# Adaptive max pooling: a full load of 64 KB rows comes first, the short load of 8 KB rows second

## The chip, the cores and the metric

The kernel runs on one core of a Trainium2 chip. The metric is the device time in microseconds (us) of one execution; the median of three runs is 335.33 us. All data is float32. Of the core's engines only VectorE (DVE in the profile) computes; SyncE (SP) and ScalarE (ACT) issue transfers, which 16 DMA engines carry out.

## The reference

```python
batch, channels, length = 32, 256, 4096
output_size = 256

def reference(x, output_size):
    result = np.zeros((batch, channels, output_size), dtype=np.float32)
    for i in range(output_size):
        start = int(i * length / output_size)
        end = int((i + 1) * length / output_size)
        result[:, :, i] = np.max(x[:, :, start:end], axis=-1)
    return result
```

The length is a multiple of the output size, so every output is the maximum of a window of 16 consecutive numbers. 134.2 MB are read and 8.4 MB written, each once.

## The kernel before

The input is seen as 2,097,152 windows of 16 floats (64 bytes each), and the 128 partitions share them: 16,384 windows a partition. They form two groups. In group A each partition owns 15,436 consecutive windows, in group B 948 (`last`).

Group A is loaded in pieces, and the list `group_a` (line 42) gives their sizes in windows a partition: 972, then fourteen of 1024 (`CHUNK`), then 128 (`FIRST`). The loop of line 79 takes the list backwards, and the position `a` goes down with it: so the first transfer is the short load, 128 partitions with rows of 128 x 64 = 8,192 bytes each, from the end of each partition's stretch. Fourteen full loads with rows of 65,536 bytes follow, then the one of 972 windows, then group B's 948. This text counts the loads of line 95 as load 0, load 1 and so on; the short load of line 86 is not among them. All are issued by SyncE, in the order of the program, into one queue.

The tile `ring` has two halves of 1176 windows (`CHUNK + GAP`), and the loads of line 95 take them in turn. Inside its half a load lies at the bottom (windows 0 to 1023) or 152 windows higher (windows 152 to 1175, `moved`): loads 0 and 1 at the bottom, loads 2 and 3 higher, loads 4 and 5 at the bottom again. The short load goes to windows 1024 to 1151 of the first half, above load 0.

VectorE reduces what has landed, in the order of the program: each load of 1024 windows in two instructions of line 55, one of 872 windows and one of 152. The first covers the windows that the load after next will overwrite, so the load after next waits for it and not for the second. Load 2, which lies over windows 152 to 1175 of the first half, also overwrites the place of the short load, so it waits for the short load's reduction too. Each load is waited for by its own semaphore.

The maxima of group A go to the tile `kept`. When all of it is there, SyncE issues one large store of it (line 115). The last load's 948 maxima overwrite the end of its own place in `ring`, and ScalarE issues their small store (line 112).

Of the kernel before, what the change touches and what calls it, by code (L numbers as in the profile page):

```python
# [1 line left out]

# [4 lines left out]


@with_exitstack
def kernel(  # L10
    ctx: ExitStack,
    tc: tile.TileContext,
    x: bass.AP,
    output_size: bass.AP,
    out: bass.AP,
):

    nc = tc.nc
    P = nc.NUM_PARTITIONS
    fp32 = mybir.dt.float32

    B, C, L = x.shape
    O = int(output_size)  # L30
    assert L % O == 0, (L, O)
    W = L // O
    total = B * C * O // P
    assert B * C * O % P == 0

    CHUNK = 1024
    GAP = 152
    FIRST = 128
    LOADS = 14

    last = 948
    group_a = [total - last - LOADS * CHUNK - FIRST] + [CHUNK] * LOADS + [FIRST]
    group_b = [last]
    assert FIRST < group_a[0] <= CHUNK and last * (W + 1) <= CHUNK * W

    pool = ctx.enter_context(tc.tile_pool(name="pool", bufs=1))
    ring = pool.tile([P, 2 * (CHUNK + GAP) * W], fp32, tag="ring", name="ring")
    kept = pool.tile([P, total - last], fp32, tag="kept", name="kept")

    xw = x.flatten_outer_dims().rearrange("r (o w) -> (r o) w", w=W)  # L50
    ow = out.flatten_outer_dims().rearrange("r o -> (r o)")

    def pooled(dst, at, n):

        nc.vector.reduce_max(  # L55
            out=dst,
            in_=ring[:, at * W : (at + n) * W].rearrange("p (n w) -> p n w", w=W),
            axis=mybir.AxisListType.X,
        )

    taken = 0

    def group(n):

        nonlocal taken
        span = slice(taken * P, (taken + n) * P)
        taken += n
        return (
            xw[span].rearrange("(p n) w -> p (n w)", p=P),
            ow[span].rearrange("(p n) -> p n", p=P),  # L70
        )

    stores = []
    n_loads = 0
    base = 0
    for g, loads in enumerate((group_a, group_b)):
        xg, og = group(sum(loads))
        a = sum(loads) if g == 0 else 0
        for n in loads[::-1]:
            if g == 0:  # L80
                a -= n
            xn = xg[:, a * W : (a + n) * W]
            dst = kept[:, base + a : base + a + n] if n != last else None
            if n == FIRST:

                nc.sync.dma_start(  # L86
                    out=ring[:, CHUNK * W : (CHUNK + n) * W], in_=xn
                )
                pooled(dst, CHUNK, n)
            else:  # L90

                low = n_loads % 2 * (CHUNK + GAP)
                moved = n_loads // 2 % 2
                at = low + moved * GAP
                nc.sync.dma_start(out=ring[:, at * W : (at + n) * W], in_=xn)  # L95
                if n != last:
                    cut = CHUNK - GAP if moved else GAP
                    parts = [(0, cut), (cut, n)]
                    for u, v in parts if moved else parts[::-1]:
                        pooled(dst[:, u:v], at + u, v - u)  # L100
                else:
                    end = (at + CHUNK) * W
                    last_kept = ring[:, end - n : end]
                    pooled(last_kept, at, n)
                n_loads += 1
            if g:
                a += n
        if g == 0:
            stores.append((og, kept[:, :]))
    assert taken == total  # L110

    nc.scalar.dma_start(out=og, in_=last_kept)
    tc.no_sync_barrier()
    for dst, src in stores:
        nc.sync.dma_start(out=dst, in_=src)


# [1 line left out]
_INS = ['x', 'output_size']  # L119
_OUTS = [((32, 256, 256), 'float32')]  # L120

_NUMBERS = {'output_size': 256}


# [26 lines left out]
```

## Time and profile before

| what | value |
|---|---|
| median of 3 runs | 335.33 us (335.17 to 335.75) |
| the profiled execution | 335.17 us, of which the span from first to last instruction is 333.4 us |
| VectorE: one full load in two instructions | 17.28 us |
| short load, from issue to landing | 4.7 us |
| full load, from issue to landing (median of 14) | 24.0 us |
| mean rate over the span | 428 GB/s |
| VectorE idle before reductions, waiting for loads | 52.2 us in 17 waits |

The profile shows one execution, with times in microseconds from the start of the span. Its page gives the busy time of each engine, then the span in 40 equal slices in which each digit is the busy share in tenths; then the DMA queues with packets, megabytes and the time of their packets as a share of the time of 16 engines. `L55` is line 55 of the kernel. `SPq` and `ACTq` stand for the instructions with which SyncE and ScalarE issue transfers. `kept<-ring 128x872 f32<-128x13952 f32` is an instruction that writes 872 numbers on each of 128 partitions from 13,952. The chain is the work that ended last, followed back from the last instruction, at each step to what released it.

### The profile page before, as it was taken

To read this page: it belongs to the slowest core of one execution; us is meant where nothing else is said; L and a number is where in the kernel's file an instruction comes from. 1 tells how busy PE (TensorE), PEld (TensorE's weight loads), DVE (VectorE), ACT (ScalarE), POOL (GpSimd) and SP (SyncE) were. 2 spreads that over 40 slices of the span, in tenths; PEclk is the share of its full clock that TensorE was granted. 3 is DMA by queue.
4 is the path that set the end of the run, shared out by engine and by line. 5 is a ranking of instruction groups with operands and counts; after the bars stand their busy time and mean duration, and the time that the engine had idled before them with its cause. 6 is when DMAs were issued, how large, how long until landed. Compare 5 with 4: busy or idle time off the path is not lost.

```text
span 333.4 us, 112 instructions
## 1 busy us (share of the span) xinstructions
DVE 276.6 (83%) x32; POOL 0.2 (0%) x4
## 2 busy tenths in 40 slices
DVE  2009979797997979799797979989797998989894
POOL 0000000000000000000000000000000000000000
DMA  9898989899898989899898989899998989999987
GB/s 377 377 503 377 503 377 503 377 425 456 377 503 377 503 377 503 377 456 425 377 503 377 503 377 503 377 488 393 393 488 377 503 377 478 411 417 466 450 378 295
DMA packets 2736, 142.61 MB, mean 428 GB/s; under 512 B 304, under 2 KB 304, under 8 KB 432
## 3 DMA queue, kind: packets, MB, share of 16 engines
q1 hardware_dynamic: 2592, 142.12, 98.7%
q10 hardware_dynamic: 144, 0.49, 0.5%
HBM read 134.22 MB, written 8.39 MB: 428 GB/s over the span
## 4 chain that ended last, share of the span: by engine, by line
DMA 62%; DVE 36%; SPq 0%; issue 0%; DVEq 0%
DMA ring<-in_x_dram 62%; DVE kept L55 31%; DVE ring L55 5%; SPq L95 0%; SPq L86 0%; DVEq L55 0%
## 5 line engine op out<-in xcount | busy, mean ns | idle before, releaser
L55 DVE TENSOR_REDUCE kept<-ring 128x872 f32<-128x13952 f32 (+3 forms) x31 | 260.6, 8447 | 50.5 <-DMA ring<-in_x_dram 50.5
L55 DVE TENSOR_REDUCE ring<-ring 128x948 f32<-128x15168 f32 x1 | 16.0, 15953 | 1.6 <-DMA ring<-in_x_dram 1.6
L132 POOL MEMSET const-bfloat16-1.0<- 128x1 bf16 x1 | 0.1, 101 | 0.0
L132 POOL MEMSET const-uint8-127<- 128x1 uint8 x1 | 0.1, 101 | 0.0
L132 POOL MEMSET const-float32-0.0<- 128x1 f32 x1 | 0.1, 98 | 0.2 <-issue 0.2
L132 POOL MEMSET const-float32-1.0<- 128x1 f32 x1 | 0.1, 98 | 0.0
## 6 DMA issues: line engine op xcount, KB each, us to landing
ring<-in_x_dram SPq DMA_DIRECT2D x1, 7776.0 KB, 23.0
out_dram<-kept SPq DMA_DIRECT2D x1, 7718.0 KB, 19.8
ring<-in_x_dram SPq DMA_DIRECT2D x1, 7584.0 KB, 21.6
ring<-in_x_dram SPq DMA_DIRECT2D x1, 1024.0 KB, 4.7
out_dram<-ring ACTq DMA_DIRECT2D x1, 474.0 KB, 3.8
ring<-in_x_dram SPq DMA_DIRECT2D x14, 24.0
```

Of the source, the lines that this page charges most:

```text
L55: nc.vector.reduce_max(out=dst, in_=ring[:, at * W : (at + n) * W].rearrange("p (n w) -> p n w", w=W), axis=mybir.AxisListType.X,)
L132: nc = _bacc.Bacc("TRN2", target_bir_lowering=False, num_devices=1)
```

## The change

The list of sizes is built without the short load at its end, and the short load is put in ahead of the list's last element:

```diff
-    group_a = [total - last - LOADS * CHUNK - FIRST] + [CHUNK] * LOADS + [FIRST]
+    group_a = [total - last - LOADS * CHUNK - FIRST] + [CHUNK] * LOADS
+    group_a.insert(-1, FIRST)
```

Read backwards, as the loop does, the list now gives 1024, 128, then thirteen times 1024, 972. Load 0 is issued first and takes the last 1024 windows of each partition's stretch; the short load comes second and takes the 128 windows below them; load 1 and all later loads take the windows that they took before. The places in `ring` stay as they were: load 0 at windows 0 to 1023 of the first half, the short load at 1024 to 1151, load 1 at the bottom of the second half. On VectorE the order is now: load 0's two reductions, the short load's, load 1's two, and on as before. Load 2 waits, as before, for the first part of load 0's reduction and for the short load's reduction, of which the latter now comes last. The lines behind line 42 move down by one.

## The prediction

> **What bounds the kernel now.** I read the page first: the busy shares, the row of slices and the queues.
>
> ```profile
> span 333.4 us, 112 instructions
> DVE 276.6 (83%) x32; POOL 0.2 (0%) x4
> DMA  9898989899898989899898989899998989999987
> q1 hardware_dynamic: 2592, 142.12, 98.7%
> ```
>
> VectorE (DVE) works 276.6 of 333.4 us. The transfers of SyncE's queue (q1: all loads and the large store) fill 98.7% of the time of the 16 DMA engines, and no slice falls under 7 tenths. So transfers bound the kernel, and an edit costs only what makes the engines idle or slow. Next, the instructions in order of time and the chain that ended last:
>
> ```profile
> 0.73 0.36 SPq L86 DMA_DIRECT2D ring<-in_x_dram  x1
> 5.44 2.29 DVE L55 TENSOR_REDUCE kept<-ring 128x128 f32<-128x2048 f32 x1 [5.44 <-DMA ring<-in_x_dram]
> 24.79 17.28 DVE L55 TENSOR_REDUCE kept<-ring 128x872 f32<-128x13952 f32 x2 [17.06 <-DMA ring<-in_x_dram]
> 44.14 17.28 DVE L55 TENSOR_REDUCE kept<-ring 128x872 f32<-128x13952 f32 x2 [2.07 <-DMA ring<-in_x_dram]
> ...
> 311.17 0.35 SPq L115 DMA_DIRECT2D out_dram<-kept  x1
> ```
>
> ```profile
> 1.62 42.50 DMA ring<-in_x_dram
> 44.12 0.02 issue
> 44.14 14.70 DVE kept L55
> 58.84 0.02 issue
> 58.85 23.98 DMA ring<-in_x_dram
> ...
> 291.07 21.61 DMA ring<-in_x_dram
> ```
>
> In each row of the first fence the first number is the start, the second the time. Full loads land 19.35 us apart (24.79 to 44.14): 8,388,608 bytes at 433.5 GB/s. VectorE needs 17.28 us for each and waits some 2.07 us for the next. The chain names VectorE for 14.70 us of each second load because the load after next may not be issued before the first part of a reduction has freed its half of the ring; that step has cover, as the next view shows.
>
> ```profile
> 39.50 0.33 SPq L95 DMA_DIRECT2D ring<-in_x_dram  x1
> ```
>
> This is SyncE's own list around 39.5 us: the third full load (I count full loads 0, 1, 2) is issued 0.02 us after the reduction from 24.79 ends (24.79 + 14.69 = 39.48), and load 1 lands only at 44.12. So load 2 stands in the queue with a lead of 44.12 - 39.50 = 4.62 us, and the engines pass from load 1 to load 2 without a hole.
>
> **The change part by part.** Nothing is added or removed: 17 loads, 32 reductions, two stores, the same bytes, the same rows. From load 1 on the addresses in HBM are the same too. Two instructions change places: the short load (128 windows a partition, line 86) with load 0 in SyncE's queue, and the short load's reduction with load 0's two on VectorE. ScalarE and GpSimd issue nothing there, and no other queue is passed.
>
> (a) The start. Issue to reduction took 5.44 - 0.73 = 4.71 us for the short load. Its 1,048,576 bytes at 433.5 GB/s are 2.42 us, so the start cost 2.29 us. Load 0 was reduced from 24.79 = 5.44 + 19.35: it ran at full pace, and the whole ramp lies inside the short load. If the start is a fixed cost, load 0 now lands for a reduction at 0.73 + 2.29 + 19.35 = 22.37, the short load at 24.79, load 1 at 44.14: nothing gained or lost. The short load's issue comes 0.41 us later (1.14, load 0's place, instead of 0.73), which the engines, occupied with load 0 until 22, hide; without that cover it would be 0.41 us once.
>
> The trace has no cold start with 64 KB rows, so I bound it by the ramp:
>
> ```profile
> 1.50:2.00 0.50, 0.00 (x0) 0.00 (x0) 1.00 1.08 197
> 2.00:3.00 1.00, 0.00 (x0) 0.00 (x0) 1.00 0.74 254
> 3.00:4.00 1.00, 0.00 (x0) 0.00 (x0) 1.00 0.95 401
> ```
>
> These are stretches of the span, with GB/s last. Against 433.5 the missing time is 0.5 x (1 - 197/433.5) + (1 - 254/433.5) + (1 - 401/433.5) = 0.27 + 0.41 + 0.07 = 0.76 us (0.757 unrounded). If small rows alone cause it, the change gains all of it: -0.76. If instead the slowness goes by bytes, so that each engine's first row runs at 254/433.5 of the pace, a 64 KB row of 19.35/8 = 2.42 us takes 4.13, and the start loses 1.71 where it now loses the 0.41 + 0.07 of the two whole stretches: +1.23. I take 0, between: load 0's exact 19.35 us says that once a queue moves, row size costs nothing, and a fixed delay before the first bytes is the plainest reading of 197, 254, 401.
>
> (b) The new wait. Load 2 lies 152 windows higher than load 0, over windows 152 to 1176 of the half, and the short load lies at 1024 to 1152. So load 2 waits for the short load's reduction, before and after. Before, that was done at 7.7 us and cost nothing. Now it stands behind both reductions of load 0: 22.37 + 17.28 + 2.29 = 41.94 (the short load, landed at 24.79, is there when VectorE reaches it at 39.65). Load 2 is issued at 41.96, 2.46 us later than before, with a lead of 44.12 - 41.96 = 2.16 us in place of 4.62. Behind it on SyncE stands only load 3, which waits for load 1's reduction at 44.14 + 14.69 = 58.83 anyway; VectorE is free at 41.94, before load 1 lands.
>
> Is 2.16 us enough? The nearest row is the large store, which comes on the same queue behind the last load: issued at 311.17, that load landed at 291.07 + 21.61 = 312.68, a lead of 1.51 us.
>
> ```profile
> out_dram<-kept SPq DMA_DIRECT2D x1, 7718.0 KB, 19.8
> ```
>
> It landed at 311.17 + 19.8 = 330.97, thus 18.29 us after the load; its 7,903,232 bytes at 433.5 GB/s are 18.23. So a lead of 1.51 us left a hole of some 0.06 us. By that row load 2 costs nothing. By the next row, the cold start, it needs 2.29 us: a hole of 2.29 - 2.16 = 0.13. For loads in mid-stream the trace shows only leads like 4.62 to be enough; if all of it were needed the hole would be 2.46 us. I take 0, by the nearest row in queue and size; the ends for the range are 0 and +2.46.
>
> One rule speaks against the change here. The Trainium skill, DMA: Bandwidth & Descriptors, section Latency and other measured facts, gives HBM's access latency as 0.2 us on average but 2 us at high load, and about 0.6 us to the first byte of a transfer issued from this kind of queue. The store above writes HBM and does not show the read side. As an estimate from that page, 0.6 + 2 = 2.6 us of lead would be needed and the hole would be 0.44 us: 335.8 instead of 335.3.
>
> (c) The rest. A hole before load 2 is never made up, since every later load is chained to it at the pace of the transfers; without one, every later load, the last reductions, the store at 311.17 and the small store fall where they fell. VectorE loses its early 2.29 us and pays them at 39.65, inside the 21.77 us between load 0 (22.37) and load 1 (44.14), of which 19.57 are then used; if that cover went, up to 2.29 us would show.
>
> Sum against the profiled execution, 335.17 us (span 333.4, and 1.8 around it): 0 + 0 + 0 = 335.17. It is the lowest of the three runs (335.17, 335.33, 335.75); the median is 335.33, and I predict 335.3 for the changed kernel's median.
>
> **The rivals.**
>
> Load 2 comes too late (slower). From a needed lead of 2.16 us on, each further microsecond is one lost, once. For it: the lead really falls by more than half, and no load in the trace shows a lead so short. Against it: the store's 1.51 us. Price 0.13 us by the cold start (335.5), at most 2.46 (337.8); from a needed lead of 2.83 us on it would show as slower.
>
> Cold rows pay by the byte (slower). For it: 254 GB/s in the first whole microsecond. Against: the ramp is over by 4 us while still in the first transfer. Price +1.23: 336.6.
>
> The small rows are the ramp (faster). For it: 8 KB rows are the only data moved between 1.5 and 4 us, and that is where the rate is low. Against: first bytes need some time whatever the row. Price -0.76: 334.6; with a part of it, no measurable change.
>
> The change does nothing to the order: the builder's lists of SyncE and VectorE show load 0 ahead of the short load, so this has next to no weight; 335.3.
>
> **How the numbers follow.** A measurement of this kernel tells about 0.2% (0.67 us) from no change, so faster means below 334.66, slower above 336.0. Forecast 0.54 (0.50 within, 0.02 on each side by scatter of the runs); load 2 late 0.14 (0.10 slower, 0.04 too small to see); cold bytes 0.13 (0.11 and 0.02); ramp gone 0.18 (0.11 faster, 0.07 within); no effect 0.01. Together: faster 0.13, same 0.64, slower 0.23. The range takes in the ramp's whole gain at the low end, about 334.6, and at the top most of the cold-byte loss and a hole of up to 1.0 us, 336.3; the rest of the hole's bound is left out.
>
> **What would show it.** (a) Load 0's reduction starts near 22.37, load 1's near 44.14; a start of both 0.3 us or more away prices the ramp. (b) Load 2 is issued near 41.96, and its reduction starts 19.35 us after load 1's (63.5); more is the hole. (c) From there on reductions 19.35 us apart, the store near 311.2, the span 333.4. I am wrong if the engines idle before load 2, if the first rows of 64 KB start at a different cost, or if the time moves while these marks don't, that is, outside the span.

## The result and the profile after

The changed kernel takes 338.15 us (median of four runs, 337.40 to 338.24), the kernel before beside it 335.40 us: a ratio of 1.0076, with a 95% interval of 1.0064 to 1.0087. It is 2.75 us slower. The forecast was 335.3 us with a range of 334.6 to 336.3. The ratios from here on leave out slow runs, those over 1.5% above the fastest of the same kernel, of which there is one (341.12 us).

The page of the profiled execution (338.23 us) shows the same work in a longer span:

```profile
span 336.4 us, 112 instructions
DVE 276.5 (82%) x32; POOL 0.2 (0%) x4
DMA  9898989999999999999999999999999999999997
q1 hardware_dynamic: 2592, 142.12, 98.2%
```

VectorE's busy time has not moved (276.5 us against 276.6), nor have the packets and bytes of the queue. The slices tell almost nothing: they are as full as before or fuller, since a loss of 3 us is 0.9% of the span. The page could not have found the loss. The instructions in order of time do (start, duration, instruction):

```profile
0.73 0.37 SPq L96 DMA_DIRECT2D ring<-in_x_dram  x1
...
22.80 19.47 DVE L56 TENSOR_REDUCE kept<-ring 128x872 f32<-128x13952 f32 x3 [22.80 <-DMA ring<-in_x_dram]
44.61 17.28 DVE L56 TENSOR_REDUCE kept<-ring 128x872 f32<-128x13952 f32 x2 [2.34 <-DMA ring<-in_x_dram]
66.21 17.28 DVE L56 TENSOR_REDUCE kept<-ring 128x872 f32<-128x13952 f32 x2 [4.32 <-DMA ring<-in_x_dram]
85.55 17.28 DVE L56 TENSOR_REDUCE kept<-ring 128x872 f32<-128x13952 f32 x2 [2.06 <-DMA ring<-in_x_dram]
...
314.09 0.35 SPq L116 DMA_DIRECT2D out_dram<-kept  x1
```

In the kernel before, load 2's row was:

```profile
63.53 17.28 DVE L55 TENSOR_REDUCE kept<-ring 128x872 f32<-128x13952 f32 x2 [2.11 <-DMA ring<-in_x_dram]
```

Load 1 is reduced from 44.61, where it was 44.14: 0.47 us from the start. Load 2 follows 21.60 us after it, where it was 19.39 (63.53 before): 2.21 us in one step, and VectorE waits 4.32 us for it in place of 2.11. Load 3 follows after 19.34 us again. What is left of the 3.0 us by which the spans differ (336.4 - 333.4) is 0.3 us net, spread over later steps. SyncE's own list gives the issue of load 2, and the chain of the work that ended last gives load 1's landing and the wait that follows its reduction:

```profile
42.30 0.33 SPq L96 DMA_DIRECT2D ring<-in_x_dram  x1
```

```profile
1.62 42.96 DMA ring<-in_x_dram
44.59 0.02 issue
44.61 14.70 DVE kept L56
59.31 0.02 issue
59.32 26.20 DMA ring<-in_x_dram
```

Load 1 landed at 44.59, so load 2 had a lead of 44.59 - 42.30 = 2.29 us; before it had 4.62. Load 3, issued when load 1's first part was reduced, queues behind the late load 2: it stands in the chain with 26.20 us, against 23.98.

The stretches around the step, in GB/s in the last column (a packet counts where it starts, so single stretches jump and are no rates). The kernel before:

```profile
43.00:44.00 1.00, 0.00 (x0) 0.00 (x0) 1.00 2.45 1049
44.00:45.00 1.00, 0.86 (x1) 0.00 (x0) 1.00 0.00 0
45.00:46.00 1.00, 1.00 (x1) 0.00 (x0) 1.00 1.37 590
46.00:47.00 1.00, 1.00 (x1) 0.00 (x0) 1.00 1.06 459
```

And the changed kernel:

```profile
43.00:44.00 1.00, 0.00 (x0) 0.00 (x0) 1.00 1.34 524
44.00:45.00 1.00, 0.39 (x1) 0.00 (x0) 1.00 0.53 197
45.00:46.00 1.00, 1.00 (x1) 0.00 (x0) 1.00 0.90 328
46.00:47.00 1.00, 1.00 (x1) 0.00 (x0) 1.00 1.57 590
```

The four add up to 2098 before and 1639 after, which is 32 rows of 65,536 bytes begun against 25. The packet records, which hold the start and duration of each row, show why: load 1's last rows end between 43.4 and 44.2 us. Nine engines begin load 2 at once; seven begin only between 44.5 and 45.8, that is 2.2 to 3.5 us after its issue, though the first engine had begun 1.07 us after it. The first rows took up to 3.25 us, against 2.42 for a row in mid-stream. The first engine ends load 1 0.8 us ahead of the last; in load 2 this is 2.3 us. Load 2 lands at 66.2, behind its last engine's end at 65.8.

### The profile page after: what moved, and what is told of

It is laid out like the page before. It is cut to its first block, busy times and chain, and to the rows that moved or that the text cites. A ratio compares the mean times of both kernels' runs of the same rounds, so it can differ in the third digit from the quotient of the medians.

```text
span 336.4 us, 112 instructions
## 1 busy us (share of the span) xinstructions
DVE 276.5 (82%) x32; POOL 0.2 (0%) x4
## 4 chain that ended last, share of the span: by engine, by line
DMA 63%; DVE 35%; SPq 0%; issue 0%; DVEq 0%
DMA ring<-in_x_dram 63%; DVE kept L56 31%; DVE ring L56 5%; SPq L87 0%; SPq L96 0%; DVEq L56 0%
```

## The experiments

Two things had changed at once: the start (first rows of 64 KB) and the lead of load 2. Theory L says that the lead is what costs. The first two kernels part them.

**The new order, with an early load 2** (ratios here and below are to the kernel before, run beside each; the lines of code here are set against the changed kernel).

```diff
+    TOP = CHUNK + GAP + CHUNK
-                    out=ring[:, CHUNK * W : (CHUNK + n) * W], in_=xn
+                    out=ring[:, TOP * W : (TOP + n) * W], in_=xn
-                pooled(dst, CHUNK, n)
+                pooled(dst, TOP, n)
```

> The new order of transfers stays, but the short load lies at the top of the other half of the ring, so that load 2 waits only for the first part of load 0's reduction. Theory L (the lead of load 2 decides, and a first row of 64 KB costs some 0.47 us at the start): load 0 reduced from 22.8, load 1 from 44.6, load 2 issued near 37.5 with a lead of 7.1 us, reduced from 63.95, that is 19.35 after load 1; span 333.9, ratio 1.0014. Rival R (the order of rows itself puts the 16 engines out of step and that is the loss): load 2's reduction still 21.6 us after load 1's, span 336.4, ratio 1.008.

Ratio 1.0007 (0.9997 to 1.0018), median 335.87 us. Issue and reductions:

```profile
22.81 19.47 DVE L57 TENSOR_REDUCE kept<-ring 128x872 f32<-128x13952 f32 x3 [22.81 <-DMA ring<-in_x_dram]
37.53 22.13 SPq L97 DMA_DIRECT2D ring<-in_x_dram  x2
44.62 17.28 DVE L57 TENSOR_REDUCE kept<-ring 128x872 f32<-128x13952 f32 x2 [2.33 <-DMA ring<-in_x_dram]
63.97 14.69 DVE L57 TENSOR_REDUCE kept<-ring 128x872 f32<-128x13952 f32 x1 [2.08 <-DMA ring<-in_x_dram]
```

With the order of the change kept and load 2 issued at 37.53, the step from load 1 to load 2 is 19.35 us. The hole is gone; load 1's 44.62 is still there. So the order costs 0.48 us in this view, which the ratio cannot tell from nothing, and the rest comes from the wait. Rival R falls.

**The old order, with a late load 2.**

```diff
-                    for u, v in parts if moved else parts[::-1]:
+                    for u, v in parts if moved or n_loads == 0 else parts[::-1]:
```

> The old order of transfers stays, short load first; only load 0's two reductions change places, so that load 2 is issued after both, near 42.1 (24.79 + 17.28) in place of 39.50, with a lead of 2.0 us. Theory L: a hole of 2.3 us before load 2 (reduced from about 65.8 in place of 63.53), nothing else; span 335.7, ratio 1.007. Rival R, and the forecast's reading that 1.51 us is lead enough: no hole, 333.4, ratio 1.000.

Ratio 1.0068 (1.0037 to 1.0100), over nine runs between 335.92 and 340.24 us, median 338.14; a tenth took 341.12. The profiled execution was one of the shortest, 335.92:

```profile
41.97 17.09 SPq L95 DMA_DIRECT2D ring<-in_x_dram  x2
44.02 17.28 DVE L55 TENSOR_REDUCE kept<-ring 128x872 f32<-128x13952 f32 x2 [2.07 <-DMA ring<-in_x_dram]
64.08 14.69 DVE L55 TENSOR_REDUCE kept<-ring 128x872 f32<-128x13952 f32 x1 [2.79 <-DMA ring<-in_x_dram]
```

Its step is 20.06 us, a hole of 0.71 at a lead of 2.03. A late load 2 costs time without any change of order. But the size differs from execution to execution, which no theory had said, so I had the kernel profiled once more.

> The kernel with the old order and a late load 2 once more, for another profiled execution, since its times lay between 335.9 and 341.1 us and the one profiled was 335.92. Theory L with a hole that differs from execution to execution: in this one the step from load 1's reduction to load 2's is another, 20 to 25 us, and the span is 333.4 us plus what the step has over 19.35. Rival (the surplus of the slow executions lies elsewhere, in other loads or outside the span): a step near 20.06 as in the first profile, whatever the time.

```profile
42.19 17.09 SPq L95 DMA_DIRECT2D ring<-in_x_dram  x2
44.24 17.28 DVE L55 TENSOR_REDUCE kept<-ring 128x872 f32<-128x13952 f32 x2 [2.08 <-DMA ring<-in_x_dram]
66.21 14.69 DVE L55 TENSOR_REDUCE kept<-ring 128x872 f32<-128x13952 f32 x1 [4.70 <-DMA ring<-in_x_dram]
```

338.78 us, span 337.0. With the same lead, 2.03 us, the step was 21.97: a hole of 2.62 us. The two loads behind it lost another 0.36 and 0.18, together 3.16 of the 3.6 us over the span before. The surplus is where theory L puts it, and its size differs from execution to execution. In the three profiles with a lead of 2.0 to 2.3 us the hole goes with how far apart the engines end load 2 by the packet records: 0.8 us apart at a hole of 0.71, 2.3 at 2.21 (the changed kernel), 2.6 at 2.62.

**Four leads in one kernel.** In loads 0, 4, 8 and 12 a part of the second reduction goes ahead of the first.

```diff
+    EARLY = {0: 38, 4: 76, 8: 114, 12: 152}
-                    for u, v in parts if moved else parts[::-1]:
+                    parts = parts if moved else parts[::-1]
+                    early = EARLY.get(n_loads, 0)
+                    if early:
+                        parts = [(0, early), (cut, n)]
+                        if early < cut:
+                            parts.append((early, cut))
+                    for u, v in parts:
```

> The old order, with a part of load 0's, 4's, 8's and 12's second reduction (38, 76, 114 and 152 windows) put ahead of the first, so that loads 2, 6, 10 and 14 are issued later by about 0.67, 1.3, 2.0 and 2.6 us: leads of 3.95, 3.3, 2.6 and 2.0 us. Theory L with a needed lead of about 4.3 us and a loss of one for one: holes of 0.35, 1.0, 1.7 and 2.3 us in the step between the reductions, span 338.7, ratio 1.016. Theory L with a threshold (a load is either in time or some 2.2 us late): holes of 0 or about 2.2. Forecast's reading: no holes, ratio 1.000.

Ratio 1.0157 (1.0107 to 1.0208). In the profiled execution the steps of loads 2, 6, 10 and 14 lost 0.39, 1.15, 0.35 and 1.20 us (19.74, 20.50, 19.70, and 19.58 for the shorter load 14, which takes 18.38 otherwise). The ratio was guessed well, the holes were not: in this execution, the shortest of four at 338.42 us, they add up to 3.1 us in place of 5.35, and they go neither one for one with the missing lead nor by a threshold. Already at 3.9 us something is lost.

**Every load a little late.** To average over such differences, the same was done in all fourteen full loads, with 38 and with 76 windows.

```diff
+                    parts = parts if moved else parts[::-1]
+                    if n == CHUNK:
+                        u, v = parts.pop()
+                        x = EARLY
+                        parts = (
+                            [(v - x, v)] + parts + [(u, v - x)]
+                            if moved
+                            else [(u, u + x)] + parts + [(u + x, v)]
+                        )
+                    for u, v in parts:
```

> The old order; in every full load 38 windows of the second reduction are put ahead of the first, so that each of the loads 2 to 15 is issued some 0.65 us later, with a lead of about 3.95 us where it was 4.62. Theory L (each late load draws a hole of its own, by the kernel with four leads about 0.4 us at this lead, and a hole gives the next load that much more lead): a sum of 2 to 5 us over 14 loads, ratio 1.006 to 1.015. Rival O (only the first late load hurts, because it puts the engines out of step once): below 0.7 us, ratio under 1.002. The forecast's reading that 1.51 us is enough: 1.000.

> The same with 76 windows, leads of about 3.3 us. Theory L: holes of 0.4 to 1.2 us, each giving the next load more lead, a sum of 5 to 12 us, ratio 1.015 to 1.036, above the kernel with 38 windows. Rival O: under 1.3 us, ratio under 1.004. Forecast's reading: 1.000.

Ratios 1.0104 (1.0064 to 1.0143) and 1.0246 (1.0227 to 1.0266). Over 14 loads that is a mean of 0.0104 x 335.5 / 14 = 0.25 us a load with leads set to 3.95 us, and 0.59 us with 3.3. Single loads differ: in the profiled execution with 38 windows nine loads had leads of 3.92 to 3.96 us, and their holes go from 0 to 0.7 us; the last load, with a lead of 3.35 us, lost another 1.5. Rival O, that only the first late load hurts, falls. In the kernel with 76 windows one sees how a hole pays for most of the next load, which then has that much more lead:

```profile
63.55 17.34 DVE L56 TENSOR_REDUCE kept<-ring 128x76 f32<-128x1216 f32 x3 [2.10 <-DMA ring<-in_x_dram]
84.14 17.34 DVE L56 TENSOR_REDUCE kept<-ring 128x76 f32<-128x1216 f32 x3 [3.25 <-DMA ring<-in_x_dram]
103.50 17.34 DVE L56 TENSOR_REDUCE kept<-ring 128x76 f32<-128x1216 f32 x3 [2.02 <-DMA ring<-in_x_dram]
125.02 17.34 DVE L56 TENSOR_REDUCE kept<-ring 128x76 f32<-128x1216 f32 x3 [4.18 <-DMA ring<-in_x_dram]
144.58 17.34 DVE L56 TENSOR_REDUCE kept<-ring 128x76 f32<-128x1216 f32 x3 [2.22 <-DMA ring<-in_x_dram]
```

Steps of 20.59, 19.36, 21.52 and 19.56 us. The last of them is 0.2 us too long although its load had a lead of 5.46 us (issued at 119.54, the load ahead landed at 125.00); the engines were 3.3 us apart by then.

**Load 2 issued after load 1 has landed.** 128 windows of load 0 are reduced a second time, only to delay it.

```diff
+                    if n_loads == 0:
+                        pooled(dst[:, n - FIRST : n], at + n - FIRST, FIRST)
```

(with the exchanged reductions of the second kernel)

> As the old order with a late load 2, and 128 windows of load 0 are reduced a second time in between, so that load 2 is issued near 44.3, after load 1 has landed: a lead of -0.2 us. If a hole is the shortfall in lead one for one (needed lead about 4.3), it is 4.5 us, ratio 1.0135, 1.5 times that with a lead of 2.05. If an empty queue starts again in the 2.29 to 2.75 us of the kernel's own starts, the hole is 2.5 to 3.0 us, ratio 1.0075 to 1.009, no worse than with a lead of 2.05, where the other engines' traffic makes the first rows slow.

Ratio 1.0094 (1.0079 to 1.0109), runs from 338.38 to 339.05. Load 2 was issued at 44.37, 0.3 us after load 1 had landed, and reduced from 66.51. All 16 engines began it between 0.95 and 1.6 us after the issue, with first rows of 2.9 to 3.8 us, although no other load was moving. So a queue that has run dry for certain costs 3.1 us in the median (338.63 against 335.53), with little scatter in four runs. A lead of 2.03 us cost 2.7 us (338.14 against 335.44), and the intervals of the two ratios overlap: the last 2.3 us of lead before the landing bought little but scatter.

**Short rows first in the late load.**

```diff
+                m = FIRST if n_loads == 2 else n
-                nc.sync.dma_start(out=ring[:, at * W : (at + n) * W], in_=xn)
+                nc.sync.dma_start(
+                    out=ring[:, at * W : (at + m) * W], in_=xn[:, : m * W]
+                )
+                if m < n:
+                    nc.sync.dma_start(
+                        out=ring[:, (at + m) * W : (at + n) * W], in_=xn[:, m * W :]
+                    )
```

> As the kernel with the old order and a late load 2, but load 2 is two transfers, 128 windows a partition with rows of 8 KB first, then 896 with rows of 57,344 bytes, issued one after the other near 42.1 and 42.5. If any late transfer from HBM needs the same lead whatever its rows, the hole stays at 2.3 us (load 2 reduced from about 65.8), ratio 1.007. If it is rows of 64 KB that start slowly, the hole falls to some 1.0 us or less, ratio 1.003 or under.

Ratio 1.0077 (1.0058 to 1.0097), median 338.43. Rows of 8 KB at the head of a late load did not help (the exchanged reductions of the second kernel are in this one too, and in the next). The profiled execution, again a short one at 336.39, shows 0.56 us of hole at load 2 and 0.8 at the last load.

**A late load 2 from ScalarE's queue.**

```diff
+                queue = nc.scalar if n_loads == 2 else nc.sync
-                nc.sync.dma_start(out=ring[:, at * W : (at + n) * W], in_=xn)
+                queue.dma_start(out=ring[:, at * W : (at + n) * W], in_=xn)
```

> As the old order with a late load 2 (lead 2.05 us), but load 2 is issued by ScalarE on its own queue, which is empty, instead of behind load 1 in SyncE's. If the hole belongs to a queue that runs empty, or to the place behind another transfer in one queue, it changes: under 1 us in the median, ratio under 1.003. If it belongs to starting a read from HBM late, whatever the queue, it stays: median near 338.5, ratio 1.005 to 1.010, with a scatter of some us.

Ratio 1.0163 (1.0132 to 1.0194), neither. The kernel mixes two things. Load 3 came on SyncE's queue at 58.73 while load 2 was still moving on the other, the two shared the engines, load 2 was reduced only from 70.64, and load 4, which waits for that, came late in its turn. As a test of the queue its time decides nothing. The packet records of the profiled execution tell a little more: load 2's first rows began 1.4 to 3.1 us after the issue here too, and the engine that was last had ended its first row at 48.5 us. Seven more at the 2.42 us that its rows took until load 3's came between would have ended load 2 near 65.5, an estimate, which is a hole of some 2.4 us. Another queue was no remedy in this execution.

**The short load as a cushion.** Load 0, load 1, short load, load 2; load 2 is issued as late as in the second kernel, with 2.42 us more work queued ahead of it (the lines are set against the changed kernel; not shown are the exchanged reductions and the argument with which `pooled` reads the other tile).

```diff
+    group_a.insert(-2, FIRST)
-                nc.sync.dma_start(
-                    out=ring[:, CHUNK * W : (CHUNK + n) * W], in_=xn
-                )
-                pooled(dst, CHUNK, n)
+                nc.sync.dma_start(out=kept[:, : n * W], in_=xn)
+                pooled(dst, 0, n, kept)
```

> Load 0 comes first, load 1 second, the short load third (into a part of the result tile that is written only at the end), load 2 fourth; load 0's two reductions stay exchanged, so that load 2 is issued as late as in the other kernels with a late load 2, 17.3 us after load 0's landing (near 40.1). Only the work queued ahead of it is longer, by the short load's 2.42 us: a lead of some 4.4 us against the end of what is queued. Theory L: no hole; load 2 reduced 19.35 + 2.42 us after load 1 (near 42.2 and 63.97), span 333.9, ratio 1.0014, small scatter. Rival T (the instant of issue or the exchanged reductions hurt, not the length of the queue): hole of 0.7 to 5 us, ratio near 1.007, scatter of some us.

```profile
40.32 17.09 SPq L94 DMA_DIRECT2D ring<-in_x_dram  x2
42.37 17.28 DVE L56 TENSOR_REDUCE kept<-ring 128x872 f32<-128x13952 f32 x2 [2.07 <-DMA ring<-in_x_dram]
59.56 2.27 DVE L56 TENSOR_REDUCE kept<-kept 128x128 f32<-128x2048 f32 x1
64.20 14.69 DVE L56 TENSOR_REDUCE kept<-ring 128x872 f32<-128x13952 f32 x1 [2.36 <-DMA ring<-in_x_dram]
```

Ratio 1.0012 (1.0003 to 1.0021), runs from 335.67 to 336.38. Load 2 came 2.03 us ahead of load 1's landing, just as in the second kernel, and the step is 21.83 us, of which 19.35 and 2.42 are the two transfers: no hole, at a lead of 2.03 + 2.42 = 4.45 us over the end of the queued work. Not the instant of issue and not the exchanged reductions cost time, but how much is queued ahead.

**A start with rows of 2 KB.**

```diff
+    TINY = 32
+                for u, v in ((0, TINY), (TINY, n)):
+                    nc.sync.dma_start(
+                        out=ring[:, (CHUNK + u) * W : (CHUNK + v) * W],
+                        in_=xn[:, u * W : v * W],
+                    )
```

> The kernel before, with its short load in two transfers: 32 windows (rows of 2 KB) first, then 96 (rows of 6 KB). If the cost of the start goes with the length of the first rows (64 KB rows landed load 1 at 44.6, rows of 8 KB at 44.1), load 1 is reduced from 44.0 or earlier, ratio 0.9990 to 0.9997. If the start has a floor that 8 KB rows have reached, or the second issue of 0.41 us starves the engines, 44.1 to 44.5, ratio 1.000 to 1.001.

Ratio 1.0006 (0.9997 to 1.0014), load 1 reduced from 44.22. Rows under 8 KB gain nothing. In this execution the last load landed 0.6 us late (18.65 us after its predecessor). A possible reason, argued and not shown, stands in the kernel before: its last load is issued at 291.07 and the one ahead of it landed by 294.71, a lead of only 3.64 us, because that one is shorter (972 windows). Other kernels took from 17.99 us (the new order with an early load 2) to 18.87 us (short rows first) for this step at the same lead.

**The last load with a full lead.** The load of 972 windows goes to the front, and the large store is split so that it has a lead too (not shown is the assertion that goes with the list).

```diff
-    group_a = [total - last - LOADS * CHUNK - FIRST] + [CHUNK] * LOADS + [FIRST]
+    odd = total - last - LOADS * CHUNK - FIRST
+    group_a = [CHUNK] * LOADS + [odd, FIRST]
-            stores.append((og, kept[:, :]))
+            stores.append((og[:, CHUNK:], kept[:, CHUNK:]))
+            stores.append((og[:, :CHUNK], kept[:, :CHUNK]))
```

> The kernel before, with the odd load of 972 windows directly behind the short load instead of next to last, so that the last load is issued with a lead of 4.62 us where it had 3.64, and with the large store in two (the part that is complete one load earlier first, then the last 1024 maxima a partition), so that the store has its lead too. Theory L: the step of the last load is 18.0 us in each execution (it was 18.05 to 18.9 in kernels whose other loads were in time), the scatter of the runs is smaller and the median 0.1 to 0.4 us lower, ratio 0.999 to 1.000. Rival (the scatter of the kernel before has another cause): ratio 1.000 and the same scatter of some 1.5 us; a loss of up to 0.5 us if rows of 4 KB at the end of the store cost something.

Ratio 0.9985 (0.9976 to 0.9994): 335.06 us against 335.45, eleven runs between 334.77 and 335.13 where the kernel before, beside it, has 335.30 to 335.72. It beats both kernels. But the last load's step was 18.18 us here, over the 18.0 expected and over the 18.05 of the kernel before, so the profiles do not show the gain at that load. Which share the last load's lead, the store's and the changed order of the loads have in it was not tried.

## Why the prediction was wrong

The chain of events was foreseen, its price was not.

(a) The start, taken as 0 with bounds of -0.76 and +1.23, cost 0.47 us by load 1's reduction (44.61 for 44.14). First rows of 64 KB took 2.8 to 3.5 us, against 2.42 in mid-stream. A fixed cost of the start was the wrong reading, but the 0.47 us lie inside the bounds and alone would have left the time within 0.2% (ratio 1.0007). The bounds themselves were weak: 197, 254 and 401 GB/s were taken as rates, but a packet counts where it starts, and the stretch from 4 to 5 us has 1147 (the missing time worked out from them is 0.762 us unrounded, not 0.757).

(b) The wait was right to some tenths: load 2 issued at 42.30 (forecast 41.96), lead 2.29 us (2.16). **The step that failed is "By that row load 2 costs nothing".** The row was the large store, with a lead of 1.51 us and a hole of 0.06. In the changed kernel the store behaves in the same way: the packet records show its first rows on all engines 0.85 to 1.4 us after the issue, at nearly their full pace (2.28 to 2.32 us for 2.28). Load 2, with more lead than that, lost 2.2 us. The store reads SBUF and writes HBM, the load reads HBM; the prediction named that difference beside the rule of the skill, and then went by the row that was nearest in queue and size. The row nearest in direction would have been the start of the kernel itself, but it too gave only 0.13 us. Even the start with 64 KB rows, which needed 22.80 - 0.73 - 19.35 = 2.72 us in the changed kernel, would have given no more than 2.72 - 2.29 = 0.43 us.

The upper bound of that term, +2.46 us for the case that the whole lead of 4.62 us is needed, was close to what came. Leads of 4.45 us and more cost nothing in most steps and up to 0.24 us in single ones (19.59 us once in the last kernel), a little more where the engines were far apart; leads set to 3.95 us cost a mean of 0.25 a load, 3.3 a mean of 0.59, and 2.0 to 2.3 cost 0.7 to 2.6 in three executions. That bound was on the page, and the range then left most of it out ("a hole of up to 1.0 us"). That it came so near is partly luck: the loss does not grow one for one with the missing lead, as the rival had it, since load 2 issued 0.3 us after load 1's landing lost 3.1 us and not 4.9. The slower rival, Load 2 comes too late, with its point of decision and its 2.46 us at most, was what happened, except that a microsecond of lead is not a microsecond of loss; it had a chance of 0.14.

The rule that was weighed, from the Trainium skill, DMA: Bandwidth & Descriptors, Latency and other measured facts (2 us to reach HBM at high load), points the right way. The estimate of 0.44 us worked out from it is five times too small against the 2.2 us measured.

(c) That a hole is never made up held: from load 3 on the steps are 19.35 us again, with some tenths lost on the way. The rival that the small rows are the ramp falls (without them at the head load 1 came 0.47 us later, not 0.76 earlier), the one of cold bytes holds in sign, at 0.47 in place of 1.23 us.

Two things stay open. What makes single engines late: the records do not tell whether their descriptors or their first bytes from HBM came late. And why the engines end load 2 only 0.8 us apart in one execution and 2.6 in another at the same lead, with losses of 0.7 and 2.6 us.

## What to carry to other kernels

In a kernel bound by its loads, treat the lead of each transfer over the end of the queued work as a resource with a measured need, which lies here between 3.95 us (up to 0.7 us lost) and 4.45 us (nothing lost) for reads of 8 MB, and recompute it for every transfer whose wait an edit moves; where the trace shows only one lead to be enough, count the whole loss below it as possible. The store that restarted quickly said nothing about a load. A piece of another size shortens or lengthens the lead of the transfers around it, so put it where they keep theirs; a small independent transfer queued ahead of a late one made a cushion here.

## What was not expected of the hardware

A load issued 2.03 us before the load ahead had landed cost nearly as much in the median as one issued 0.3 us after (2.7 and 3.1 us), but with far more scatter (nine runs from 335.92 to 340.24 us against four from 338.38 to 339.05). The engines can leave such a start out of step, in the changed kernel 2.3 us apart where they were 0.8 us, and keep this for many loads: there they were still 1.5 us apart ten loads later.
